# Up projection with tokens on partitions, turned back by block transposes on VectorE

## The chip, the cores and the metric

The kernel runs on one core of one Trainium2 chip. The metric is the device time of one execution in microseconds (us). Before the change, three runs took 2050.69, 2050.99 and 2053.95 us; the median is 2050.99 us. A core has five engines with queues of their own, each working its instructions in order: TensorE (PE, matrix products; its weight loads are shown as PEld), VectorE (DVE), ScalarE (ACT), GpSimd (POOL) and SyncE (SP), which here issues the DMA transfers of the weights. Engines wait for one another by semaphores.

## The reference

One layer of a streaming encoder is computed for 384 tokens: a prompt of 256 frames and 8 streams of 16 new frames. The change lies in the last part, a feed-forward block with a gate and a short convolution over time:

```python
h2 = rmsnorm(x, norm_ffn_g)
up = h2 @ w_up                       # 2048 -> 2 * 5632
g_half = up[..., :D_FF]
u_half = up[..., D_FF:]
ext_f = jnp.concatenate([ffn_buf.astype(g_half.dtype), g_half], axis=1)
gc = causal_dwconv(ext_f, ffn_dw_w, ffn_dw_b)     # 3 taps along time
x = x + (jax.nn.silu(gc) * u_half) @ w_down       # 5632 -> 2048
new_ffn = ext_f[:, -(FFN_CONV_W - 1):]
```

The row factor of `rmsnorm` is one number per token. It commutes with the projection, so the kernel multiplies it in behind the matmuls; the factors of `norm_ffn_g` are in the activations already.

## The kernel before

All matrix products are taken in split precision. A weight tile `raw` (128 partitions × 2 × 512 fp32 numbers, that is two contraction steps of 128 rows and 512 columns) is fetched by SyncE (`fetch`, L117). ScalarE rounds it to `hi` (L124) and VectorE subtracts to get the rest, `lo` (L125). Activations are kept as such a pair too. Each product is three matmuls: hi·hi, hi·lo and lo·hi. `raw` has three buffers, `hi` and `lo` two each. In this document a weight pair is one such tile: two contraction steps.

`gemm` runs jobs. A job makes 512 output columns over `nk` contraction steps, in one of two kinds:

- kind A: the weights are the stationary operand, 128 columns of them at a time, and the 384 tokens stream past. Four PSUM tiles of 128 features × 384 tokens come out: features on partitions. A step takes 4 × 3 = 12 matmuls of 384 columns.
- kind B: the activations are the stationary operand, 128 tokens at a time, and 512 weight columns stream past. Three PSUM tiles of 128 tokens × 512 features come out: tokens on partitions. A step takes 3 × 3 = 9 matmuls of 512 columns.

PSUM has five tiles for this (`acc`). At the job's last step its `evac` functions read the PSUM tiles, and `done` puts further work behind them. The order of TensorE is that of the program; the other engines' orders come from a scheduler that gives the weight splits (`SPLIT_AHEAD`) and the evacuations (`EVAC_AHEAD`) precedence over the rest, so that splits stand between the instructions of an evacuation on VectorE and ScalarE.

The feed-forward part runs 11 groups of 512 features. `up_jobs(g)` gives two jobs of 16 steps (8 weight pairs) each, both kind A: the g job (gate half) and the u job (other half). After some groups come the down jobs (`down_jobs`, kind B) of the groups that are done: `FFN_PLAN` runs five groups up, four down, four up, four down, two up and the last three down.

In the g job's evacuation VectorE multiplies each PSUM tile by the row factors `rs2` (L871), which have been spread over all partitions by matmuls with ones (`over_partitions`, L283), and writes it into `extf`: 24 pieces of 16 tokens, each with two places ahead of it for the two tokens before. GpSimd fills these places, from the neighbouring piece (L873) or from the stored state `sfT` (L874). Then VectorE makes the three taps (L888 for the first, L890 for the other two), ScalarE applies SiLU (L892), GpSimd multiplies by the row factors of the other half (L893) and copies the last tokens for the new state (L894). In the u job VectorE multiplies the PSUM tile by that gate (L910), ScalarE rounds the product to `hi` (L912) and VectorE subtracts to get `lo` (L913): the activations of the down projection.

Of the kernel before, what the change touches and what calls it, by code (L numbers as in the profile page):

```python
# [8 lines left out]
F32 = mybir.dt.float32  # L9
F32R = mybir.dt.float32r  # L10
AF = mybir.ActivationFunctionType
# [4 lines left out]
P = 128  # L16
# [23 lines left out]
def hybrid_step(  # L40
# [33 lines left out]
    def f(ap):  # L74
        return ap.bitcast(F32)
# [34 lines left out]

    # ------------------------------------------------------------------ weight streaming
    def fetch(srcs):
# [51 lines left out]
    def after(units, fn):  # L164
        later.append([units, fn])
# [216 lines left out]

    # ------------------------------------------------------------------ log forget gates
    def tiny(name):
# [61 lines left out]

    # ------------------------------------------------------------------ q, k norms
    def head_rsqrt(a):
# [19 lines left out]

    # ------------------------------------------------------------------ attention
    p_att, close_att = pool("att", side="right")  # L470
# [136 lines left out]

    # ------------------------------------------------------------------ GLU
    ut = gp.tile([P, 8, NT], F32, tag="G4", name="ut")
# [80 lines left out]

    # ------------------------------------------------------------------ gates, conv branch
    p_hl, close_hl = pool("attHL", side="right")
# [20 lines left out]

    # ------------------------------------------------------------------ LayerNorm + swish, att_out
    def layer_norm():
# [60 lines left out]

    # ------------------------------------------------------------------ pointwise, mix
    mix = [gp.tile([P, 2, 4, NT], F32R, tag=f"G{g}", name=f"mix{g}") for g in range(4)]
# [18 lines left out]

    # ------------------------------------------------------------------ w_out, residual, second norm
    p_r, close_r = pool("resid", side="right")
    y = p_r.tile([P, NTT, DM], F32, name="y")  # L800
    xg = [p_r.tile([P, 2, 4, NT], F32R, name=f"xg{g}") for g in range(4)]
    rs2 = p_r.tile([P, NT], F32, name="rs2")
    ss2 = p_r.tile([P, NTT, 4], F32, name="ss2")
# [29 lines left out]
    def second_norm():  # L833
        m2 = p_f.tile([P, NTT], F32, name="m2")
        nc.vector.tensor_reduce(m2[:], ss2[:], axis=mybir.AxisListType.X, op=ALU.add)
        ts(m2[:], m2[:], 1.0 / DM, EPS, op0=ALU.mult, op1=ALU.add)
        r2 = rsqrt(m2[:], [P, NTT], p_f, "r2")
        dg = diagonals(p_f, r2, "r2")
        after(2, lambda: over_partitions(dg, rs2[:]))

    gemm([job("B", 16, grouped(mix), wo_evac(n), done=wo_done(n)) for n in range(4)])

    # ------------------------------------------------------------------ FFN
    sfT = p_f.tile([P, 44, 16], F32, name="sfT")
    sfv = sfT[:].rearrange("p (c i) r -> p c i r", i=11)
    sf_in = state_ffn[0].rearrange("b r (c p) -> (b r c) p", p=P).rearrange("(q i) p -> q i p", i=11)
    for u, i0 in enumerate(range(0, 11, 3)):
# [11 lines left out]
        after(2 + 2 * u, ffn_state)  # L859
    extf = [p_f.tile([P, 24, 18], F32, name=f"extf{m}") for m in range(4)]  # L860
    for m in range(4):
        nc.gpsimd.memset(extf[m][:, 0, 0:2], 0.0)
    xa = grouped(xg)
    acts = {}

    def up_g_evac(g, sg):
        def ev(m, ps):
            c = 4 * g + m
            e = extf[m]
            v = e[:, :, 2:18]  # L870
            tt(v, ps[:, :NT].rearrange("p (a t) -> p a t", t=16), rs2[:].rearrange("p (a t) -> p a t", t=16),  # L871
               op=ALU.mult)
            nc.gpsimd.tensor_copy(e[:, 1:16, 0:2], e[:, 0:15, 16:18])  # L873
            nc.gpsimd.tensor_copy(e[:, 16:24, 0:2], sfT[:, c, :].rearrange("p (b r) -> p b r", r=2))  # L874
        return ev

    def up_g_done(g, sg):
        def done():
            gcs = [p_f.tile([P, NT], F32, tag="gc", bufs=4, name="gc") for _ in range(4)]
            lc = p_f.tile([P, 18, 4], F32, tag="lc", bufs=2, name="lc")  # L880
            for w in range(3):
                for m in range(4):
                    c = 4 * g + m
                    o = gcs[m][:].rearrange("p (a t) -> p a t", t=16)
                    v = extf[m][:, :, w:w + 16]
                    wc = fw[:, w * 44 + c:w * 44 + c + 1]
                    if w == 0:
                        ts(o, v, wc, col[:, R_FDB + c:R_FDB + c + 1], op0=ALU.mult, op1=ALU.add)  # L888
                    else:
                        stt(o, v, wc, o, op0=ALU.mult, op1=ALU.add)  # L890
            for m in range(4):
                nc.scalar.activation(gcs[m][:], gcs[m][:], AF.Silu)  # L892
                nc.gpsimd.tensor_tensor(sg[m][:], gcs[m][:], rs2[:], op=ALU.mult)  # L893
                nc.gpsimd.tensor_copy(lc[:, :, m].rearrange("p (a r) -> p a r", r=2), extf[m][:, 15:24, 16:18])  # L894

            def new_state():
                ps = misc_tile()
                tr(ps[:72, :P], lc[:].rearrange("p a m -> p (a m)"), ident[:])
                nf = p_f.tile([72, P], F32, tag="nf", bufs=2, name="nf")
                nc.scalar.copy(nf[:], ps[:72, :P])  # L900
                cs = slice(512 * g, 512 * (g + 1))
                nc.sync.dma_start(prompt_ffn[0, 0, :, cs].rearrange("r (m p) -> r m p", m=4), nf[0:8, :])
                nc.sync.dma_start(sample_ffn[0, :, :, cs].rearrange("b r (m p) -> (b r) m p", m=4), nf[8:72, :])
            after(10, new_state)
        return done

    def up_u_evac(g, sg):
        def ev(m, ps):
            a = p_f.tile([P, NT], F32, tag="ac", bufs=2, name="ac")
            tt(a[:], ps[:, :NT], sg[m][:], op=ALU.mult)  # L910
            hi, lo = acts[g][:, 0, m, :], acts[g][:, 1, m, :]
            nc.scalar.copy(hi, a[:])  # L912
            tt(lo, a[:], f(hi), op=ALU.subtract)  # L913
        return ev

    def up_jobs(g):
        sg = [p_f.tile([P, NT], F32, tag="sg", bufs=6, name="sg") for _ in range(4)]
        acts[g] = gp.tile([P, 2, 4, NT], F32R, tag=f"G{g % 5}", name=f"act{g}")
        return [job("A", 16, xa, up_g_evac(g, sg), done=up_g_done(g, sg)), job("A", 16, xa, up_u_evac(g, sg))]

# [59 lines left out]
```

## Time and profile before

| what | value |
|---|---|
| median of three runs | 2050.99 us |
| span of the profiled execution, first to last instruction | 2050.9 us |
| TensorE busy | 2035.2 us (99%) |
| VectorE busy | 1046.1 us (51%) |
| ScalarE busy | 723.9 us (35%) |
| GpSimd busy | 225.8 us (11%) |
| moved by DMA | 276.19 MB, mean 135 GB/s |
| matmuls of the up projection, 384 columns | 3 lines (L203 to L205) × 1408 |
| matmuls of the down projection, 512 columns | 3 lines (L208 to L210) × 528 |
| mean clock granted to TensorE | 0.998 of full speed |

The profiled execution's time is its span, 2050.9 us, which stands within 0.1 us of the median: next to nothing lies around it. A row of a group of instructions reads: line, engine, operation, output <- inputs by the program's names, shapes, count | busy us in all, mean ns of one | idle time of the engine just before them, and what ended most of it. A row of a timeline reads: start in us from the span's start, length, engine, line, operation, and in brackets the idle time before it and what ended it. Several like instructions in a row are merged, with their count; the length is then from the first one's start to the last one's end. Instructions of one engine overlap: one can start before the last one's end, and a few records of matmuls can be missing.

### The profile page before, as it was taken

Reading aid. Unit: us, or ns where it says so; the run is one execution under the profiler, and the core shown is the slowest. Engines: PE = TensorE matmul, PEld = TensorE weight load, DVE = VectorE, ACT = ScalarE, POOL = GpSimd, SP = SyncE. Lnnn points to the kernel's source line nnn. Section 1 sums busy time; section 2 is a strip of 40 time slices with the busy share of each in tenths; the row PEclk is TensorE's granted clock in tenths of the full one; section 3 lists DMA queues with packets and bytes.
Section 4 is the critical chain, followed back from the end, with each engine's and each line's share of the span. In section 5 each row is a group of like instructions: output and inputs, shape, how many; then the busy total and the mean of one; then the engine's idle time right before and its main releaser. Section 6 shows DMA issues by size and latency. Waiting matters only on the chain.

```text
span 2050.9 us, 27732 instructions
## 1 busy us (share of the span) xinstructions
PE 2035.2 (99%) x11198; PEld 1909.6 (93%) x11198; DVE 1046.1 (51%) x1413; ACT 723.9 (35%) x1071; POOL 225.8 (11%) x309
## 2 busy tenths in 40 slices
PE   8999999999999999999999999999999999999999
PEld 8988999999999999888999999888999998899987
DVE  4434477778872556344544454433544453335443
ACT  5334455433333433333322332222323332223222
POOL 2000011112120013000221122000220120002100
PEclk9999999999999999999999999999999999999999
DMA  6555465344444344534444444444444444444443
GB/s 179 170 168 159 146 166 162 101 127 119 127 125 125 122 124 125 201 124 121 121 130 124 128 131 124 129 128 133 126 124 130 128 124 133 124 134 124 126 152 124
DMA packets 171214, 276.19 MB, mean 135 GB/s; under 512 B 10841, under 2 KB 58224, under 8 KB 170694
## 3 DMA queue, kind: packets, MB, share of 16 engines
q1 hardware_dynamic: 170542, 273.62, 44.8%
q8 instruction: 87, 1.43, 0.3%
q0 software_dynamic: 512, 0.80, 0.2%
q14 instruction: 41, 0.34, 0.0%
q10 hardware_dynamic: 32, 0.01, 0.0%
HBM read 266.98 MB, written 7.86 MB: 134 GB/s over the span
## 4 chain that ended last, share of the span: by engine, by line
PE 96%; DVE 2%; POOL 1%; DMA 1%; ACT 0%; issue 0%; POOLq 0%; ACTq 0%
PE acc L205 20%; PE acc L203 20%; PE acc L204 20%; PE acc L209 11%; PE acc L210 11%; PE acc L208 11%; DVE ut L663 1%; DVE lo L125 1%; DMA raw<-in_w_in_dram 1%; POOL sgA L710 1%; PE misc L513 0%; PE misc L819 0%; PE misc L579 0%; PE misc L546 0%; POOL sgB L710 0%
## 5 line engine op out<-in xcount | busy, mean ns | idle before, releaser
L125 DVE TENSOR_TENSOR lo<-raw,hi 128x1024 fp32r<-128x1024 f32 (+1 forms) x480 | 588.4, 1226 | 899.3 <-ACT hi L124 894.1
L124 ACT CAST hi<-raw 128x1024 fp32r<-128x1024 f32 (+1 forms) x480 | 497.8, 1037 | 1127.6 <-PE acc L204 665.1
L203 PE MATMUL acc<-xg,hi 128*128 128x384 f32 x1408 | 474.9, 337 | 0.0
L205 PE MATMUL acc<-xg,lo 128*128 128x384 f32 x1408 | 473.1, 336 | 0.0
L204 PE MATMUL acc<-xg,hi 128*128 128x384 f32 x1408 | 473.1, 336 | 0.0
L203 PEld LDWEIGHTS acc<-xg,hi 128*128 128x128 f32 x1408 | 264.7, 188 | 1.4
L204 PEld LDWEIGHTS acc<-xg,hi 128*128 128x128 f32 x1408 | 264.8, 188 | 0.1
L205 PEld LDWEIGHTS acc<-xg,lo 128*128 128x128 f32 x1408 | 264.7, 188 | 0.0
L205 PE MATMUL acc<-hT,lo 128*128 128x384 f32 x768 | 259.8, 338 | 4.8 <-DVE lo L125 4.8
L203 PE MATMUL acc<-hT,hi 128*128 128x384 f32 x768 | 262.5, 342 | 0.0
L204 PE MATMUL acc<-hT,hi 128*128 128x384 f32 x768 | 257.7, 336 | 0.0
L209 PE MATMUL acc<-lo,act 128*128 128x512 f32 x528 | 205.4, 389 | 0.0
L210 PE MATMUL acc<-hi,act 128*128 128x512 f32 x528 | 205.4, 389 | 0.0
L208 PE MATMUL acc<-hi,act 128*128 128x512 f32 x528 | 205.4, 389 | 0.0
L663 DVE SCALAR_TENSOR_TENSOR ut<-ext,cw,ut 128x384 f32<-128x384 f32 x240 | 165.2, 688 | 6.1
L205 PEld LDWEIGHTS acc<-hT,lo 128*128 128x128 f32 x768 | 144.7, 188 | 9.2 <-DVE lo L125 8.5
L203 PEld LDWEIGHTS acc<-hT,hi 128*128 128x128 f32 x768 | 144.7, 188 | 2.2 <-issue 1.4
L204 PEld LDWEIGHTS acc<-hT,hi 128*128 128x128 f32 x768 | 144.9, 189 | 0.0
L208 PE MATMUL acc<-hi,hT 128*128 128x512 f32 (+1 forms) x336 | 123.0, 366 | 2.9 <-ACT hi L124 2.9
L209 PE MATMUL acc<-lo,hT 128*128 128x512 f32 (+1 forms) x336 | 121.4, 361 | 0.7 <-DVE lo L125 0.7
L210 PE MATMUL acc<-hi,hT 128*128 128x512 f32 (+1 forms) x336 | 121.4, 361 | 0.0
L208 PEld LDWEIGHTS acc<-hi,act 128*128 128x128 f32 x528 | 99.1, 188 | 20.7
(290 smaller groups left out, 2119.8 us busy)
## 6 DMA issues: line engine op xcount, KB each, us to landing
raw<-in_w_up_dram SPq DMA_DIRECT2D x176, 512.0 KB
raw<-in_w_in_dram SPq DMA_DIRECT2D x96, 512.0 KB
raw<-in_w_down_dram SPq DMA_DIRECT2D x88, 512.0 KB
raw<-in_w_in_dram SPq DMA_DIRECT2D x64, 256.0 KB
raw<-in_w_out_dram SPq DMA_DIRECT2D x32, 512.0 KB
raw<-in_w_in_dram SPq DMA_DIRECT2D x24, 344.0 KB
raw<-in_w_att_out_dram SPq DMA_DIRECT2D x16, 512.0 KB
raw<-in_conv_pw_out_dram SPq DMA_DIRECT2D x16, 512.0 KB
```

The costliest lines, as they stand in the source:

```text
L124: nc.scalar.copy(hi[:, :, :o], raw[:, :, :o])
L125: tt(lo[:, :, :o], raw[:, :, :o], f(hi[:, :, :o]), op=ALU.subtract)
L203: mm(o, hi[:, kk, s], ah, start=st, stop=False)
L204: mm(o, hi[:, kk, s], al, start=False, stop=False)
L205: mm(o, lo[:, kk, s], ah, start=False, stop=sp)
L208: mm(o, ah[:, s], hi[:, kk, :n], start=st, stop=False)
L209: mm(o, ah[:, s], lo[:, kk, :n], start=False, stop=False)
L210: mm(o, al[:, s], hi[:, kk, :n], start=False, stop=sp)
L663: stt(o, v, wc, o, op0=ALU.mult, op1=ALU.add)
L710: nc.gpsimd.tensor_tensor(d, d, rs1b[:], op=ALU.mult)
```

## The change

Both up jobs become kind B. ScalarE evacuates each PSUM tile (128 tokens × 512 features) into a buffer `tok` in SBUF and multiplies by the row factor on the way, which is now a number per partition; `rs2` shrinks to one column per 128 tokens and isn't spread over partitions any more. Since both halves get their factor there, L893 goes. Then VectorE turns `tok` into features on partitions. Its transpose works on square blocks of 32 × 32: one instruction reads 32 partitions (32 tokens of each of the three token tiles, in 4 × 3 blocks) and writes 32 other partitions; 16 of them, 4 quarters of the features × 4 quarters of the tokens, turn one job's tile. The g half is written into `extf`, the u half into a new buffer `uT`. The work behind stays: carried tokens on GpSimd, taps on VectorE, SiLU, product, split. `extf` is one tile for the four feature blocks in place of four tiles, and `tok` and `uT` have one buffer each.

```diff
@@ second_norm @@
         r2 = rsqrt(m2[:], [P, NTT], p_f, "r2")
-        dg = diagonals(p_f, r2, "r2")
-        after(2, lambda: over_partitions(dg, rs2[:]))
+        nc.vector.tensor_copy(rs2[:], r2[:])
@@ FFN @@
-    extf = [p_f.tile([P, 24, 18], F32, name=f"extf{m}") for m in range(4)]
+    extf = p_f.tile([P, 4, 24, 18], F32, name="extf")
...
-    def up_g_evac(g, sg):
-        def ev(m, ps):
-            c = 4 * g + m
-            e = extf[m]
-            v = e[:, :, 2:18]
-            tt(v, ps[:, :NT].rearrange("p (a t) -> p a t", t=16), rs2[:].rearrange("p (a t) -> p a t", t=16),
-               op=ALU.mult)
-            nc.gpsimd.tensor_copy(e[:, 1:16, 0:2], e[:, 0:15, 16:18])
-            nc.gpsimd.tensor_copy(e[:, 16:24, 0:2], sfT[:, c, :].rearrange("p (b r) -> p b r", r=2))
+    def tok_rows():
+        return p_f.tile([P, NTT, 512], F32, tag="tok", bufs=1, name="tok")
+
+    def up_evac(rows):
+        def ev(t, ps):
+            nc.scalar.activation(rows[:, t, :], ps[:], AF.Identity, scale=rs2[:, t:t + 1])
         return ev
 
-    def up_g_done(g, sg):
+    def blocks(rows, put):
+        src = rows[:].rearrange("p t (m b j) -> p b m t j", m=4, b=4)
+        for b in range(4):
+            for a in range(4):
+                nc.vector.transpose(put(a, slice(32 * b, 32 * b + 32)), src[32 * a:32 * a + 32, b])
+
+    def up_g_done(g, rows, sg):
         def done():
+            def put(a, js):
+                return extf[js].rearrange("p m (t a) c -> p m t a c", t=NTT)[:, :, :, 2 * a:2 * a + 2, 2:18]
+
+            blocks(rows, put)
...
+            for m in range(4):
+                e = extf[:, m]
+                nc.gpsimd.tensor_copy(e[:, 1:16, 0:2], e[:, 0:15, 16:18])
+                nc.gpsimd.tensor_copy(e[:, 16:24, 0:2], sfT[:, 4 * g + m, :].rearrange("p (b r) -> p b r", r=2))
...
             for m in range(4):
-                nc.scalar.activation(gcs[m][:], gcs[m][:], AF.Silu)
-                nc.gpsimd.tensor_tensor(sg[m][:], gcs[m][:], rs2[:], op=ALU.mult)
-                nc.gpsimd.tensor_copy(lc[:, :, m].rearrange("p (a r) -> p a r", r=2), extf[m][:, 15:24, 16:18])
+                nc.scalar.activation(sg[m][:], gcs[m][:], AF.Silu)
+                nc.gpsimd.tensor_copy(lc[:, :, m].rearrange("p (a r) -> p a r", r=2), extf[:, m, 15:24, 16:18])
...
-    def up_u_evac(g, sg):
-        def ev(m, ps):
-            a = p_f.tile([P, NT], F32, tag="ac", bufs=2, name="ac")
-            tt(a[:], ps[:, :NT], sg[m][:], op=ALU.mult)
-            hi, lo = acts[g][:, 0, m, :], acts[g][:, 1, m, :]
-            nc.scalar.copy(hi, a[:])
-            tt(lo, a[:], f(hi), op=ALU.subtract)
-        return ev
+    def up_u_done(g, rows, sg):
+        def done():
+            uT = p_f.tile([P, 4, NT], F32, tag="uT", bufs=1, name="uT")
+            blocks(rows, lambda a, js: uT[js].rearrange("p m (t a i) -> p m t a i", t=NTT, a=4)[:, :, :, a])
+            for m in range(4):
+                tt(uT[:, m], uT[:, m], sg[m][:], op=ALU.mult)
+                hi, lo = acts[g][:, 0, m, :], acts[g][:, 1, m, :]
+                nc.scalar.copy(hi, uT[:, m])
+                tt(lo, uT[:, m], f(hi), op=ALU.subtract)
+        return done
 
     def up_jobs(g):
...
-        return [job("A", 16, xa, up_g_evac(g, sg), done=up_g_done(g, sg)), job("A", 16, xa, up_u_evac(g, sg))]
+        gr, ur = tok_rows(), tok_rows()
+        return [job("B", 16, xa, up_evac(gr), done=up_g_done(g, gr, sg)),
+                job("B", 16, xa, up_evac(ur), done=up_u_done(g, ur, sg))]
```

In the changed file the lines that follow have new numbers: the evacuation is L870, the transposes L877, GpSimd's copies L889 (from the neighbouring piece), L890 (from the stored state) and L903 (for the new state), the taps L898 (first) and L900, SiLU L902, the product L921, its rounding L923 and its rest L924.

More of the change, by code (lines that the diff above doesn't have):

```diff
@@ L801, in hybrid_step @@
     xg = [p_r.tile([P, 2, 4, NT], F32R, name=f"xg{g}") for g in range(4)]
-    rs2 = p_r.tile([P, NT], F32, name="rs2")
+    rs2 = p_r.tile([P, NTT], F32, name="rs2")
     ss2 = p_r.tile([P, NTT, 4], F32, name="ss2")
@@ L859, in hybrid_step @@
         after(2 + 2 * u, ffn_state)
-    extf = [p_f.tile([P, 24, 18], F32, name=f"extf{m}") for m in range(4)]
+    extf = p_f.tile([P, 4, 24, 18], F32, name="extf")
     for m in range(4):
-        nc.gpsimd.memset(extf[m][:, 0, 0:2], 0.0)
+        nc.gpsimd.memset(extf[:, m, 0, 0:2], 0.0)
     xa = grouped(xg)
     acts = {}
-    def up_g_evac(g, sg):
-        def ev(m, ps):
-            c = 4 * g + m
-            e = extf[m]
-            v = e[:, :, 2:18]
-            tt(v, ps[:, :NT].rearrange("p (a t) -> p a t", t=16), rs2[:].rearrange("p (a t) -> p a t", t=16),
-               op=ALU.mult)
-            nc.gpsimd.tensor_copy(e[:, 1:16, 0:2], e[:, 0:15, 16:18])
-            nc.gpsimd.tensor_copy(e[:, 16:24, 0:2], sfT[:, c, :].rearrange("p (b r) -> p b r", r=2))
-        return ev
-    def up_g_done(g, sg):
+    def tok_rows():
[3 more added lines that the diff above has]
+            nc.scalar.activation(rows[:, t, :], ps[:], AF.Identity, scale=rs2[:, t:t + 1])
+        return ev
+    def blocks(rows, put):
[4 more added lines that the diff above has]
+    def up_g_done(g, rows, sg):
         def done():
+            def put(a, js):
+                return extf[js].rearrange("p m (t a) c -> p m t a c", t=NTT)[:, :, :, 2 * a:2 * a + 2, 2:18]
+            blocks(rows, put)
+            lc = p_f.tile([P, 18, 4], F32, tag="lc", bufs=2, name="lc")
             gcs = [p_f.tile([P, NT], F32, tag="gc", bufs=4, name="gc") for _ in range(4)]
-            lc = p_f.tile([P, 18, 4], F32, tag="lc", bufs=2, name="lc")
+            for m in range(4):
+                e = extf[:, m]
+                nc.gpsimd.tensor_copy(e[:, 1:16, 0:2], e[:, 0:15, 16:18])
+                nc.gpsimd.tensor_copy(e[:, 16:24, 0:2], sfT[:, 4 * g + m, :].rearrange("p (b r) -> p b r", r=2))
             for w in range(3):
@@ L884, in done @@
                     o = gcs[m][:].rearrange("p (a t) -> p a t", t=16)
-                    v = extf[m][:, :, w:w + 16]
+                    v = extf[:, m, :, w:w + 16]
                     wc = fw[:, w * 44 + c:w * 44 + c + 1]
```

## The prediction

> **What bounds the kernel now.** I read the page's first table, then the chain of waits, then the timeline of each engine around one group of the up projection, and last the groups of instructions by shape.
>
> ```profile
> PE 2035.2 (99%) x11198; PEld 1909.6 (93%) x11198; DVE 1046.1 (51%) x1413; ACT 723.9 (35%) x1071; POOL 225.8 (11%) x309
> ...
> PE 96%; DVE 2%; POOL 1%; DMA 1%; ACT 0%; issue 0%; POOLq 0%; ACTq 0%
> ...
> SPq L117 <- DVE lo L125: 827.1, 228, 4.6
> ```
>
> TensorE (PE) bounds it: 99% busy, 96% of the chain. In the up stage it never waits, so what counts is how fast matmuls follow one another and whether another engine makes it late. The last row is from the waits of the DMA queue: it waits for VectorE (DVE) to free a weight buffer, so the weights come early and DMA has room.
>
> The timeline of TensorE gives the pace, first in the up projection (384 columns), then in a down projection (512 columns):
>
> ```profile
> 1252.25 0.34 PE L205 MATMUL acc<-xg,lo 128*128 128x384 f32 x1
> 1252.43 0.34 PE L203 MATMUL acc<-xg,hi 128*128 128x384 f32 x1
> 1252.60 0.34 PE L204 MATMUL acc<-xg,hi 128*128 128x384 f32 x1
> ...
> 1323.89 0.39 PE L210 MATMUL acc<-hi,act 128*128 128x512 f32 x1
> 1324.12 0.39 PE L208 MATMUL acc<-hi,act 128*128 128x512 f32 x1
> 1324.35 0.39 PE L209 MATMUL acc<-lo,act 128*128 128x512 f32 x1
> ```
>
> Starts are 0.173 us apart with 384 columns and 0.227 with 512. The durations overlap; only the distance of starts counts. The difference, 0.0533 us for 128 columns, makes 0.160 for 384, so every matmul also carries about 0.013 us that doesn't depend on its width.
>
> The timeline of VectorE (then ScalarE, ACT) shows the clock that each weight pair keeps. One pair is one 512 KB fetch, two contraction steps:
>
> ```profile
> 1184.25 1.23 DVE L125 TENSOR_TENSOR lo<-raw,hi 128x1024 fp32r<-128x1024 f32 x1 [2.94 <-ACT hi L124]
> 1185.94 2.12 DVE L871 TENSOR_TENSOR extf<-acc,rs 128x384 f32<-128x384 f32 x4 [0.46 <-PE acc L205]
> 1187.97 0.47 DVE L888 TENSOR_SCALAR gc<-extf,fw,col 128x384 f32<-128x384 f32 x1
> 1188.41 1.23 DVE L125 TENSOR_TENSOR lo<-raw,hi 128x1024 fp32r<-128x1024 f32 x1
> 1189.56 1.25 DVE L888 TENSOR_SCALAR gc<-extf,fw,col 128x384 f32<-128x384 f32 x3
> 1190.72 2.20 DVE L890 SCALAR_TENSOR_TENSOR gc<-extf,fw,gc 128x384 f32<-128x384 f32 x4
> 1192.84 1.22 DVE L125 TENSOR_TENSOR lo<-raw,hi 128x1024 fp32r<-128x1024 f32 x1
> 1193.98 2.98 DVE L890 SCALAR_TENSOR_TENSOR gc<-extf,fw,gc 128x384 f32<-128x384 f32 x4
> 1197.25 1.67 DVE L125 TENSOR_TENSOR lo<-raw,hi 128x1024 fp32r<-128x1024 f32 x1 [0.29 <-ACT hi L124]
> ...
> 1242.62 1.23 DVE L125 TENSOR_TENSOR lo<-raw,hi 128x1024 fp32r<-128x1024 f32 x1 [2.93 <-ACT hi L124]
> 1246.78 1.23 DVE L125 TENSOR_TENSOR lo<-raw,hi 128x1024 fp32r<-128x1024 f32 x1 [2.94 <-ACT hi L124]
> ...
> 1324.32 1.05 ACT L124 CAST hi<-raw 128x1024 fp32r<-128x1024 f32 x1 [3.02 <-PE acc L210]
> ...
> 1325.40 1.22 DVE L125 TENSOR_TENSOR lo<-raw,hi 128x1024 fp32r<-128x1024 f32 x1 [2.85 <-ACT hi L124]
> 1329.49 1.23 DVE L125 TENSOR_TENSOR lo<-raw,hi 128x1024 fp32r<-128x1024 f32 x1 [2.86 <-ACT hi L124]
> ```
>
> A pair takes 4.16 us in the up projection (24 matmuls of 0.1733) and 4.08 in the down projection (18 of 0.2267). The first nine rows are the burst at a job's end: VectorE works it off between the splits of L125 and no split comes too late. That room is what the change spends. The casts and splits run one pair ahead, since `hi` and `lo` have two buffers: the cast for the next pair starts 0.20 us after this pair's first matmul (1324.32 against 1324.12), its split 1.08 later, and is done 2.51 us after that matmul.
>
> **The change, part by part.** *Matmuls.* All 22 up jobs go from 12 matmuls of 384 columns a step to 9 of 512: the same columns, a quarter fewer matmuls. With 8 pairs a job that is 176 pairs × (4.16 − 4.08) = **−14.1 us**, all on the bounding engine.
>
> *Norm scale.* `over_partitions` goes from the second norm:
>
> ```profile
> 978.09 0.34 PE L205 MATMUL acc<-xg,lo 128*128 128x384 f32 x1
> 978.27 0.83 PE L283 MATMUL misc<-r2d,ones 128*128 128x128 f32 x6
> ...
> 979.12 0.34 PE L204 MATMUL acc<-xg,hi 128*128 128x384 f32 x1
> ```
>
> L204 came 1.03 us after L205 where two steps of 0.173 would do: **−0.7 us**. The small VectorE and ScalarE work beside it was hidden.
>
> *Evacuation.* Six ScalarE activations of 128x512 a group replace L871 and the PSUM read of L910. The groups by shape give all prices:
>
> ```profile
> L871 DVE TENSOR_TENSOR extf<-acc,rs 128x384 f32<-128x384 f32 x44 | 23.3, 558 | 5.1 <-PE acc L205 5.1
> L927 DVE TENSOR_TENSOR y<-acc,y 128x512 f32<-128x512 f32 x36 | 24.6, 692 | 9.0 <-PE acc L210 9.0
> L890 DVE SCALAR_TENSOR_TENSOR gc<-extf,fw,gc 128x384 f32<-128x384 f32 x88 | 56.1, 700 | 0.0
> L893 POOL TENSOR_TENSOR sg<-gc,rs 128x384 f32<-128x384 f32 x44 | 59.9, 1390 | 12.6 <-ACT gc L892 12.6
> L370 ACT ACTIVATE kt<-acc,rs 128x512 f32<-128x512 f32 x4 | 2.7, 680 | 3.3 <-PE acc L210 3.3
> ```
>
> 0.68 us each, the third behind the cast of pair 1, so it ends at 0.23 + 1.05 + 0.68, about 1.9 us after the next job's first matmul. VectorE is then still in the split of pair 1 (until 2.51), which hides it; without that cover the block transposes would start up to 0.6 us earlier, no more. ScalarE idles 3 us a pair (bracket of its row), so its casts stay punctual. The next job has its three PSUM tiles free: five exist, three are used. POOL's L893 goes, off the path.
>
> *The transposes.* This is the cost: 16 of 32 partitions × 384 elements in each job, 352 in all, on VectorE. No row of before shows one. In the changed program VectorE's order after a job is: split 1, 7 transposes, split 2, 6 transposes, split 3, 3 transposes, then in a g job the four L898, split 4, five L900, split 5; in a u job three L921, split 4, three L924, one L921, split 5. What counts is the distance from one transpose to the next.
>
> Bounds from the rows: below, the L888 rows, 0.39 apart (1.25 − 0.47 over 2), or the L871 row, 0.52 apart ((2.12 − 0.56)/3), where an instruction starts before the last has ended; above, the 0.70 of L890 plus a full serial gap. That gap shows where each VectorE instruction needs the one before:
>
> ```profile
> 40.04 0.18 DVE L99 RECIPROCAL r1r<-r1s 128x3 f32<-128x3 f32 x1 [1.15 <-ACT r1s L98]
> 40.25 0.16 DVE L100 TENSOR_TENSOR r1s<-r1r 128x3 f32<-128x3 f32 x1
> ```
>
> 0.03 us from end to start. I take a plain 384-element instruction (0.558, L871) run serially: 0.558 + 0.03 = **0.59 us**. Nearest is the chained row, because every transpose reads another quarter of the partitions than the one before, while all overlapping rows keep to the same 128; and a block must be full before its first output row exists.
>
> The walk, zero at the next job's first matmul. `lo` of pair n is needed by the second matmul of the pair, at 4.08n + 0.23 − 0.03.
> - Split 1 from 1.28; the next instruction enters 1.15 us behind it (1188.41 to 1189.56), at 2.46. Seven transposes end at 6.6.
> - Split 2, 6.6 to 7.82, needed 8.36: in time. Six transposes, 7.86 to 11.4.
> - Split 3, 11.4 to 12.63, needed 12.44: TensorE waits 0.2. Three transposes, to 14.43.
> - In a g job L898 waits for POOL's L889 copy, which waits for the last transpose:
>
> ```profile
> 1186.63 0.21 POOL L873 COPY extf<-extf 128x30 f32<-128x30 f32 x1 [52.55 <-DVE extf L871]
> ```
>
> The first L871 began at 1185.94 and lasted 0.56, so POOL began 0.13 after its end; with 0.21 and 0.03 the L898s start at 14.80, last 4 × 0.39 and split 4 runs 16.36 to 17.58. It was needed at 16.72 (shifted by the 0.2): 0.86 more. **1.06 us a g job.** The L890 copies wait only for the last group's convolution and are long done. Split 5 (20.15 to 21.37, needed 21.66) is in time again.
> - In a u job three L921 at 0.52 put split 4 at 16.0 to 17.22: 0.2 + 0.5 = **0.71 us a u job**; split 5 is in time.
>
> Eleven groups: 11 × 1.77 = **+19.5 us**. A split that is up to 2.4 us later also frees its `raw` buffer later; a fetch is issued three pairs ahead and lands inside that (SP's wait for VectorE, above, is the evidence), so I price it at nothing; the cover gone would be DMA time on TensorE at each job. Last, the final down job reads `act` of group 10 from its ninth step; the late L924 costs about 0.25 once.
>
> Sum against the profiled execution, whose span of 2050.9 is the median of the three runs (2050.99) within 0.1: 2050.9 − 14.1 − 0.7 + 19.5 + 0.25 = **2056 us**. Each 0.01 us in the transpose's distance is 16 × 0.01 a job, 22 jobs: 3.5 us. Below 0.577 us the change wins; below about 0.52 nothing waits.
>
> The Trainium skill, "VectorE: DVE Perf Modes", section "The three transpose paths", gives 311 ns for a 128×128 bf16 block transpose; an estimate from that figure, with 256 more elements at the 1.05 ns each between L871 and L927, is 0.58 us, serially 0.61, and the sum would be 2063. No run here shows it yet.
>
> **Rivals.**
> 1. *Transposes overlap* as L871 does, 0.52 us apart or less (0.54 costs little). For it: every unchained pair of VectorE rows overlaps. Against: the changing partitions. All splits are in time, 2050.9 − 14.8 = **2036 us**; decides below 0.577.
> The Trainium skill, "VectorE: DVE Perf Modes", section "Two Vector instructions with no wait between them", speaks against this rival: an instruction whose first input starts in another quarter of the partitions than the last one's is held until all before it have finished. No row of before shows such a pair.
> 2. *Near the break-even*, 0.565 to 0.589 apart: the two terms cancel, 2047 to 2055.
> 3. *Each block fills, then drains*, with no overlap inside the instruction: 384 elements cost twice 0.40 (1.05 ns each, L871 to L927), 0.96 + 0.03 = 0.99 us. Waits grow by 32 × 0.40 = 12.8 us a group, (1.77 + 12.8) × 11 = 160: **2196 us**. Nothing in the trace speaks for it but that no transpose is in it. The dear end of the rows, 0.73, gives (1.77 + 32 × 0.14) × 11 = 69: 2105.
> 4. *The matmuls gain nothing*, because the activations become the stationary side. The down rows have that form and run at 0.227; I give it no chance of its own.
>
> **How the numbers follow.** A measurement of this kernel can tell a change of about 0.2%, 4.1 us, from none. Overlapping or nearly so, up to 0.565: 0.30, faster. Near the break-even: 0.15, the same (the forecast's own edge reaches into slower at 0.589). Serial, 0.589 to 0.75: 0.40, 2055 to 2110, its likeliest part 2055 to 2070. Above that, towards rival 3: 0.15. The predicted time is that of the serial case by rows, 2056. The range 2036 to 2110 takes in the overlapping case and the dear end of the rows and leaves out 0.15 above and little below.
>
> **What would show it.** Matmuls of xg with 512 columns, 0.227 apart; the transposes at L877 and their distance, 0.59; TensorE waits ended by `lo` L125 in the third and fourth pair of each job, some 20 us in all; group time near 67.0 us (before: 16 × 4.16 = 66.6) where 65.3 would be free of waits; POOL without L893. A distance at or below 0.55 makes the prediction wrong towards 2036; one above 0.75, or splits held up by something else (POOL's copies, late fetches), makes it wrong upwards.

## The result and the profile after

The changed kernel takes 2068.68 us (median of five runs, 2066.53 to 2069.50) where the kernel before takes 2053.95 us beside it (2050.69 to 2054.38). The ratio is 1.0078, with a 95% interval of 1.0066 to 1.0089: slower, by about 16 us. The profiled execution has a span of 2064.8 us, 13.9 more than before's 2050.9.

The changed kernel's page: the busy line of each engine, the chain of waits, and the groups of the `lo` matmul in the up and in the down projection.

```profile
PE 2044.5 (99%) x10136; PEld 1767.5 (86%) x10136; DVE 1205.1 (58%) x1719; ACT 767.7 (37%) x1136; POOL 161.7 (8%) x265
...
PE 85%; DVE 10%; issue 2%; ACT 1%; POOL 1%; DMA 1%; POOLq 0%; ACTq 0%
...
L209 PE MATMUL acc<-lo,xg 128*128 128x512 f32 x1056 | 419.3, 397 | 3.8 <-DVE lo L125 3.8
...
L209 PE MATMUL acc<-lo,act 128*128 128x512 f32 x528 | 206.1, 390 | 0.2
```

TensorE has 1062 instructions fewer (10136 for 11198), and the span is longer. The chain goes through VectorE for 10% of the span (2% before): nearly all of that is the burst of transposes and what stands in line with it. And the same matmul, 512 columns of `lo` weights, lasts 397 ns with `xg` as the stationary operand and 390 with `act`. The timeline of TensorE, first in the up projection, then in a down projection, shows what that does to the distance of starts:

```profile
1182.77 0.40 PE L208 MATMUL acc<-hi,xg 128*128 128x512 f32 x1
1183.00 0.40 PE L209 MATMUL acc<-lo,xg 128*128 128x512 f32 x1
...
1184.87 0.40 PE L208 MATMUL acc<-hi,xg 128*128 128x512 f32 x1
...
1323.73 0.39 PE L210 MATMUL acc<-hi,act 128*128 128x512 f32 x1
1323.96 0.39 PE L208 MATMUL acc<-hi,act 128*128 128x512 f32 x1
...
1325.09 0.39 PE L210 MATMUL acc<-hi,act 128*128 128x512 f32 x1
```

In the up projection nine distances make 2.10 us, 0.2333 each; in the down projection six make 1.36, 0.2267. A weight pair, 18 matmuls, takes 4.20 us in the up projection and not 4.08. Before it took 4.16. So the fewer matmuls cost 176 × (4.20 − 4.16) = 7.0 us more.

VectorE's timeline in the changed kernel, the burst behind a u job's matmuls and the end of the one behind the next g job's:

```profile
1156.67 1.23 DVE L125 TENSOR_TENSOR lo<-raw,hi 128x1024 fp32r<-128x1024 f32 x1 [2.98 <-ACT hi L124]
1157.82 4.04 DVE L877 STREAM_TRANSPOSE uT<-tok 32x384 f32<-32x384 f32 x7
1161.89 1.23 DVE L125 TENSOR_TENSOR lo<-raw,hi 128x1024 fp32r<-128x1024 f32 x1
1163.15 3.49 DVE L877 STREAM_TRANSPOSE uT<-tok 32x384 f32<-32x384 f32 x6
1166.67 1.22 DVE L125 TENSOR_TENSOR lo<-raw,hi 128x1024 fp32r<-128x1024 f32 x1
...
1186.15 1.23 DVE L125 TENSOR_TENSOR lo<-raw,hi 128x1024 fp32r<-128x1024 f32 x1 [2.97 <-ACT hi L124]
1190.35 1.23 DVE L125 TENSOR_TENSOR lo<-raw,hi 128x1024 fp32r<-128x1024 f32 x1 [2.97 <-ACT hi L124]
...
1201.61 1.74 DVE L877 STREAM_TRANSPOSE extf<-tok 32x384 f32<-32x384 f32 x3
1203.73 1.72 DVE L898 TENSOR_SCALAR gc<-extf,fw,col 128x384 f32<-128x384 f32 x4 [0.38 <-POOL extf L889]
1205.37 1.21 DVE L125 TENSOR_TENSOR lo<-raw,hi 128x1024 fp32r<-128x1024 f32 x1
```

Seven transposes in 4.04 us, the next instruction right behind: they stand 0.58 apart, one after the other. Two splits 4.20 apart, 1186.15 and 1190.35, show the pair's length where nothing is late. TensorE's timeline where it waits for the last of these splits:

```profile
1205.87 0.40 PE L208 MATMUL acc<-hi,xg 128*128 128x512 f32 x1
1206.64 0.50 PE L209 MATMUL acc<-lo,xg 128*128 128x512 f32 x1 [0.38 <-DVE lo L125]
```

That is a late split: 0.77 from start to start where 0.233 would do, 0.54 lost. (The bracket counts only from the modelled end of the last matmul, so it shows less than is lost.) To add up such losses, every distance between successive up-projection matmuls that exceeds the usual one by over 0.03 us is taken, and its excess summed. In the following this sum is called the late time. It is 9.0 us in the changed kernel (49 distances) and 1.8 before (20), where no split of this stage's groups is late: 0.8 lies in the first 25 us of the stage, and one distance a group is some 0.09 too long in every kernel here. The down projection, counted in the same way, loses 1.8 us in the changed kernel (13 distances) and nothing before: the bursts of the three u jobs that a down projection follows end there.

By these rows the change costs +7.0 us by the pace of the matmuls, +7.2 and +1.8 by late operands in the up and the down projection, and −0.7 by the norm's matmuls: +15.3. From the start of the first up matmul to that of the last down matmul the traces have 1096.4 us before (949.9 to 2046.3) and 1111.9 after (948.2 to 2060.1), 15.5 more. That the span grew by only 13.9 is since the stages ahead, which are the same, took 1.7 us less in this execution; in the other runs here the first up matmul starts between 947.6 and 951.4. What was open: why a matmul of the same shape is slower with `xg`, and whether the late splits come from the transposes alone.

### The profile page after: what moved, and what is told of

Same layout as the page of the kernel before. It is cut to its first block, busy times and chain, and to the rows that moved or that the text cites. A ratio compares the mean times of both kernels' runs of the same rounds, so it can differ in the third digit from the quotient of the medians.

```text
span 2064.8 us, 25830 instructions
## 1 busy us (share of the span) xinstructions
PE 2044.5 (99%) x10136; PEld 1767.5 (86%) x10136; DVE 1205.1 (58%) x1719; ACT 767.7 (37%) x1136; POOL 161.7 (8%) x265
## 4 chain that ended last, share of the span: by engine, by line
PE 85%; DVE 10%; issue 2%; ACT 1%; POOL 1%; DMA 1%; POOLq 0%; ACTq 0%
PE acc L209 20%; PE acc L210 19%; PE acc L208 19%; PE acc L205 8%; PE acc L203 8%; PE acc L204 8%; DVE extf L877 4%; DVE lo L125 3%; DVE gc L898 1%; ACT hi L124 1%; DVE uT L877 1%; DVE ut L663 1%; DMA raw<-in_w_in_dram 1%; POOL sgA L710 1%; PE misc L513 0%
## 5 line engine op out<-in xcount | busy, mean ns | idle before, releaser
L209 PE MATMUL acc<-lo,xg 128*128 128x512 f32 x1056 | 419.3, 397 | 3.8 <-DVE lo L125 3.8
L208 PE MATMUL acc<-hi,xg 128*128 128x512 f32 x1056 | 419.3, 397 | 0.0
L210 PE MATMUL acc<-hi,xg 128*128 128x512 f32 x1056 | 417.6, 395 | 0.0
L209 PEld LDWEIGHTS acc<-lo,xg 128*128 128x128 f32 x1056 | 198.4, 188 | 56.8 <-DVE lo L125 10.6
L208 PEld LDWEIGHTS acc<-hi,xg 128*128 128x128 f32 x1056 | 198.4, 188 | 48.6
L210 PEld LDWEIGHTS acc<-hi,xg 128*128 128x128 f32 x1056 | 198.4, 188 | 47.1
L209 PEld LDWEIGHTS acc<-lo,act 128*128 128x128 f32 x528 | 99.1, 188 | 22.9 <-DVE lo L125 2.4
```

The lines of the kernel that those rows point to most:

```text
L208: mm(o, ah[:, s], hi[:, kk, :n], start=st, stop=False)
L209: mm(o, ah[:, s], lo[:, kk, :n], start=False, stop=False)
L210: mm(o, al[:, s], hi[:, kk, :n], start=False, stop=sp)
```

## Experiments

### Why the matmuls with xg are slow: its place in SBUF

In the changed kernel the program places `hi`, `lo` and `act` 96 bytes past a multiple of 128 in each partition, and `xg` at a multiple of 128. The change itself moved `xg`: `rs2`, which stands in the same pool at the far end of SBUF, shrank from 1536 bytes a partition to 12, padded to 32, and the tiles of that pool moved by the difference, 1504 bytes. The theory: the pace depends on where the two operands of a matmul lie relative to each other. The rival: on where `xg` lies by itself, or on something else in the up stage (the transposes beside it). Widening `rs2` by 8 columns moves `xg` and the other tiles at that end, the buffers of the transposes among them, by 32 bytes, and leaves the weights; widening `rs1`, which lies ahead of the weight buffers, moves these and leaves `xg` and the buffers of the transposes.

e1, `xg` moved to the weights' place:

```diff
-    rs2 = p_r.tile([P, NTT], F32, name="rs2")
+    rs2 = p_r.tile([P, NTT + 8], F32, name="rs2")
...
-        nc.vector.tensor_copy(rs2[:], r2[:])
+        nc.vector.tensor_copy(rs2[:, :NTT], r2[:])
```

> The changed kernel with rs2 eight columns wider, which moves xg (and the tiles under it) by 32 bytes in SBUF and nothing else: xg then lies at 32 bytes modulo 64, as hi, lo, mix and act do, where it lay at 0. Address theory (matmuls of xg are slow, 0.233 us apart in place of 0.227, for where xg lies): the matmuls of xg come to 0.227 apart, a weight pair to 4.08 us, 3168 x 0.0067 = 21 us less; the waits for late splits rise, because the splits are needed earlier, from about 10 to about 17 us; 2065 - 21 + 7 = 2051 in the profile. Rival, the pace belongs to the stage (its neighbours on other engines, its transfers) or to the far end of SBUF: 0.233 and 2065 as before.

e2, the weights (and `act`) moved to `xg`'s place, and e3, both moved, so that they differ again:

```diff
-    rs1 = cp.tile([P, NTT], F32, name="rs1")
+    rs1 = cp.tile([P, NTT + 8], F32, name="rs1")
...
-        nc.vector.tensor_copy(rs1[:], r[:])
+        nc.vector.tensor_copy(rs1[:, :NTT], r[:])
```

> The changed kernel with rs1 eight columns wider, which moves hi, lo, raw, mix, act and hT by 32 bytes, to 0 modulo 64; xg stays at 0. If it is the difference between the two operands' places that counts: 0.227 in the up, the down and the w_out matmuls. If a stationary operand at 0 is slow by itself: 0.233 in all of them, the down projection too. If it is neither: up 0.233, down 0.227.

> Both shifts: hi, lo, mix, act and hT at 0 modulo 64, xg at 32. Difference counts: up 0.233, down 0.227. A stationary operand at 0 is slow: up 0.227, down 0.233. Neither: up 0.233, down 0.227 as in the changed kernel, which the run before then tells from the first.

e8 and e10 are e1 with `NTT + 24` and `NTT + 16`, to see how the distance counts beyond 32 bytes:

> The changed kernel with rs2 24 columns wider, so that xg begins 64 bytes off the weights' place modulo 128 bytes and at it modulo 64. Theory of a period of 64 bytes: the up stage's matmuls are 0.227 us apart as in e1 and the time is about 2058. Rival, a period of 128 bytes (only equal places are quick): 0.233 and about 2068.

> The changed kernel with rs2 16 columns wider: xg begins 32 bytes past the weights' place modulo 128, where the changed kernel has it 32 bytes short of it (96 past). With 0.227 at distance 0 (e1), 0.229 at 64 (e8) and 0.234 at 96. Theory that the distance counts modulo 128 and is worst when odd in steps of 32: about 0.234 and 2069. Rival (it grows with the distance 0, 32, 64, 96): 0.228 and about 2061.

e9 puts the kernel before into the same difference of places, with `rs2` 8 columns wider (its uses take the first `NT` columns):

```diff
-    rs2 = p_r.tile([P, NT], F32, name="rs2")
+    rs2 = p_r.tile([P, NT + 8], F32, name="rs2")
```

> The kernel before, with rs2 8 columns wider, so that its xg begins 32 bytes off the weights' place modulo 64 bytes; there xg is the 384-column operand and the weights are loaded as 128 columns. Theory that any difference of places between the two operands slows a matmul: by 2 to 3% of the up stage's 4224 matmuls of 0.173 us, 15 to 22 us, so 2066 to 2073 us. Rival (only where the 512-column operand is the weights): 0.173 us apart as before and 2051 us.

What was measured. The place is that of `xg` less that of the weights, modulo 128 bytes; the pace is the mean distance of successive up matmuls, without those that count as late.

| kernel | columns streamed | place | pace, us | late time, us | time, us |
|---|---|---|---|---|---|
| changed | 512 | 32 | 0.2333 | 9.0 | 2068.68 |
| e1 | 512 | 0 | 0.2273 | 18.1 | 2058.49 (2055.16 to 2060.26, 8 runs) |
| e2 | 512 | 0 | 0.2272 | 18.1 | 2058.22 (one run) |
| e3 | 512 | 96 | 0.2333 | 9.0 | 2069.75 (one run) |
| e8 | 512 | 64 | 0.2291 | 15.3 | 2062.70 (one run) |
| e10 | 512 | 96 | 0.2333 | 9.2 | 2069.19 (one run) |
| before | 384 | 64 | 0.1733 | 1.8 | 2051.46 (beside e1) |
| e9 | 384 | 32 | 0.1745 | 1.8 | 2055.21 (one run; before beside it 2051.67) |

The `lo` matmul's group in e1, e8 and e10, by the pages of these kernels:

```profile
L209 PE MATMUL acc<-lo,xg 128*128 128x512 f32 x1056 | 415.6, 394 | 7.2 <-DVE lo L125 6.8
```

```profile
L209 PE MATMUL acc<-lo,xg 128*128 128x512 f32 x1056 | 417.4, 395 | 6.7 <-DVE lo L125 6.4
```

```profile
L209 PE MATMUL acc<-lo,xg 128*128 128x512 f32 x1056 | 418.9, 397 | 4.0 <-DVE lo L125 4.0
```

What follows. Moving either operand so that the places agree gives 0.227, moving both leaves 0.233: it is the difference that counts, not where `xg` lies, and e2 has the buffers of the transposes where the changed kernel has them. Equal is quick, 64 off costs about a third as much as 32 or 96 off, so the period isn't 64. That it is 128 is not shown: no kernel here has the operands an odd multiple of 128 bytes apart. (The expectation of e10 has the two sides swapped: the changed kernel is 32 past, e10 is 96 past. Both sides are equally slow.) The pace of e1 and e2 still has some of the burst in it: in e4 and e6 below, where `xg` lies as in e1 and no split of the stage's groups is late, it is 0.2268, that of the down projection. The kernel before had a difference too, 64; e9, which makes it 32, moves its pace by 0.0011, which is 4.8 us in 4224 matmuls, and its time by 3.5 us in one run, where 15 to 22 was expected of the first theory and none of the rival: neither held. So with 384 columns and the weights as the stationary operand the effect is there but small: the same step, from 64 to 32, makes 0.0042 with 512 columns and 0.0011 here. What inside the chip makes it is not settled here: no view shows the reads of the two operands.

The ratio of e1 to the kernel before is 1.0028 (1.0018 to 1.0039). Its profiled span is 2054.8 us, where 2051 was expected: the pace gained 19 us and not 21, and the late time rose by 9.1 and not 7. The direction of both is what the theory said: the pair became 0.11 us shorter, so every split's deadline moved up, and the late time went from 9.0 to 18.1. The slow matmuls had been hiding half of the burst. VectorE's timeline of e1 in the u job seen above:

```profile
1154.16 1.22 DVE L125 TENSOR_TENSOR lo<-raw,hi 128x1024 fp32r<-128x1024 f32 x1 [2.85 <-ACT hi L124]
1155.30 4.04 DVE L877 STREAM_TRANSPOSE uT<-tok 32x384 f32<-32x384 f32 x7
1159.38 1.23 DVE L125 TENSOR_TENSOR lo<-raw,hi 128x1024 fp32r<-128x1024 f32 x1
1160.63 3.49 DVE L877 STREAM_TRANSPOSE uT<-tok 32x384 f32<-32x384 f32 x6
1164.16 1.22 DVE L125 TENSOR_TENSOR lo<-raw,hi 128x1024 fp32r<-128x1024 f32 x1
```

The burst is as long as in the changed kernel (4.04 and 3.49 again). Only TensorE is quicker beside it, eight distances in 1.82 us, by its timeline:

```profile
1182.74 0.39 PE L208 MATMUL acc<-hi,xg 128*128 128x512 f32 x1
...
1184.56 0.39 PE L210 MATMUL acc<-hi,xg 128*128 128x512 f32 x1
```

### Are the late splits the transposes' doing?

e4 is e1 with the 16 transposes of a job made 4 of 128 partitions. It leaves out the exchange between quarters of the partitions (each block is turned within its own quarter); every other instruction stays.

```diff
         for b in range(4):
-            for a in range(4):
-                nc.vector.transpose(put(a, slice(32 * b, 32 * b + 32)), src[32 * a:32 * a + 32, b])
+            nc.vector.transpose(put(b, slice(0, P)), src[:, b])
```

> As e1, with 4 transposes of 128 partitions a job in place of 16 of 32: each turns its blocks within their quarter of the partitions and none goes to another quarter, so the exchange between quarters is left out and the output is not the reference's. VectorE then has 4 x 0.57 us of transposes a job in place of 16. Theory (the loss beside the matmul pace is late splits behind serial transposes): no TensorE wait in the up stage is ended by a split, and the time is 2051 - 14.1 - 0.7 = 2036. Rival (the waits come from the longer way over ScalarE, GpSimd or from the fetches): waits of some 10 us stay, 2046.

It takes 2038.13 us (2036.74 to 2039.53, four runs), ratio 0.9929 (0.9913 to 0.9946); the late time is 1.8 us, as before. Its chain of waits, by its page:

```profile
PE 96%; DVE 2%; POOL 1%; DMA 1%; ACT 0%; issue 0%; POOLq 0%; ACTq 0%
```

VectorE's share is back at before's 2%. And its groups by shape, from 1000 us on:

```profile
L876 DVE STREAM_TRANSPOSE uT<-tok 128x384 f32<-128x384 f32 x44 | 21.4, 545 | 0.0
```

A transpose of four times the elements lasts 545 ns, less than the narrow one's 569 (below): with 384 columns, 32 partitions cost no less than 128. The burst costs 2058.49 − 2038.13 = 20.4 us at the quick pace.

### Why they are serial

e5 is e1 with each transpose cut in two halves of 192 columns, which read and write the same quarters. e11 is e1 with the two loops swapped, so that four transposes in a row read the same quarter and write different ones.

```diff
-                nc.vector.transpose(put(a, slice(32 * b, 32 * b + 32)), src[32 * a:32 * a + 32, b])
+                for h in (slice(0, 2), slice(2, 4)):
+                    nc.vector.transpose(put(a, slice(32 * b, 32 * b + 32))[:, h], src[32 * a:32 * a + 32, b, h])
```

> e1 with each transpose of 32x384 cut in two of 32x192 (m = 0, 1 and m = 2, 3), 32 a job in the place of 16. Theory of the prediction (serial, each a fixed part of about 0.19 us and the rest by columns): a half takes about 0.38 us and they stand 0.39 us apart whether the next one reads the same quarter or another, 32 x 0.39 = 12.5 us a job in the place of 9.3; the splits are then later by some 20 to 50 us in all, so 2080 to 2110 us. Rival (a transpose that reads other partitions than the one before it is held, and one that reads the same ones is not): first to second half of a quarter about 0.33 us apart, across quarters 0.39.

```diff
-        for b in range(4):
-            for a in range(4):
+        for a in range(4):
+            for b in range(4):
```

> e1 with the two loops over quarters swapped: four transposes in a row read the same quarter of the partitions and write to the four others in turn. In e5 the second half of a transpose, which reads and writes the same quarters as the first, began 0.302 us after it, 0.067 before its end, and the next quarter's 0.340 us after, 0.013 past its end. Theory A (what holds a transpose is that its input starts in another quarter): twelve of fifteen stand about 0.51 us apart in the place of 0.582, the late splits fall by 0.07 x 6 each where 6 stand between two splits, about 18 to 11 us in all, and the time to about 2051. Theory B (the output's quarter holds it as well): 0.582 all through and 2058.

One of VectorE's groups by shape in e5:

```profile
L878 DVE STREAM_TRANSPOSE uT<-tok 32x192 f32<-32x192 f32 x352 | 112.0, 350 | 2.8
```

VectorE's timeline in e5, the first twelve halves behind a u job's matmuls:

```profile
1155.92 3.83 DVE L878 STREAM_TRANSPOSE uT<-tok 32x192 f32<-32x192 f32 x12
```

And the group of whole transposes in e11:

```profile
L877 DVE STREAM_TRANSPOSE uT<-tok 32x384 f32<-32x384 f32 x176 | 100.2, 569 | 2.6
```

In e5 the second half starts 0.302 us after the first (median of 330 such distances), 0.067 before its end; the next quarter's first half 0.340 after (308 distances), 0.014 past the end. The row agrees: 6 × 0.302 + 5 × 0.340 + the last's 0.32 = 3.83. So a transpose overlaps the one before if both keep to the same quarters, and is held if not. e4 agrees for whole ones: its four start at the same quarter and stand 0.46 to 0.50 us apart, less than their 0.545. In e11 the distance is 0.582 where only the output's quarter changes (median of 220) and 0.585 where both change (66), and the late time stays at 17.9 (time 2056.52 in one run): keeping the input's quarter isn't enough, a change of the output's holds it too, theory B. Each of a job's 16 transposes has a pair of quarters of its own, so every order of them is serial. For that overlap, e5's 32 instructions take 3.83 + 3.59 + 2.96 = 10.4 us a job in three stretches, where 12.5 was expected, and its time, 2059.65 us in one run (late time 20.0), is about 1 us above e1's.

### Spreading the burst

e6 is e1 with the same 16 transposes, but queued four behind each of four splits. `split` keeps its last `lo` instruction in `last_lo`; conv, gate and product come behind the fourth group, and the new state's output is moved along. Group 10's u job is left as it was.

```diff
+        def behind_split(b):
+            with tc.issue_after(last_lo[0].ins):
+                quarter(b)
+
         for b in range(4):
-            for a in range(4):
-                nc.vector.transpose(put(a, slice(32 * b, 32 * b + 32)), src[32 * a:32 * a + 32, b])
+            if spread:
+                after(2 * b + 2, lambda b=b: behind_split(b))
+            else:
+                quarter(b)
+        if spread:
+            after(9, then)
+        else:
+            then()
```

> The kernel with xg at the weights' place modulo 64 bytes (e1: matmuls 0.227 us apart, late splits 18.1 us, 2058.49 us), and each job's sixteen transposes recorded four at a time, each four queued behind the lo of one weight pair; conv, gate and product follow after the fourth group. Theory (the splits are late because 6 or 7 transposes of 0.58 us stand between two of them): four of them and a split take 4 x 0.58 + 1.22 = 3.54 us, less than a pair's 4.08, so the late time falls from 18.1 us to about 2 and the time to 2058.5 - 16 = 2042 us, up to about 4 us lower by the step that e4 measured (2038). Rival (the splits are late for another reason, the evacuation of the job on ScalarE ahead of hi, or VectorE's total work of conv and product): the late time stays near 18 us and the time near 2058.

e7 is e6 with `rs2` as the changed kernel has it, so with `xg` 32 bytes off:

> e6 with rs2 as the changed kernel has it, so that xg is again 32 bytes off the weights' place: the transposes are spread, the matmuls are not mended. Theory (two separate causes that add up): late splits about 2 us as in e6 and matmuls 0.234 us apart as in the changed kernel, 2038.7 + 3168 x 0.0067 = 2060 us, which is the changed kernel less its 9.0 us of late splits (2068.7 - 9.0 = 2059.7) and then some 2 us. Rival (the slow matmuls come from the transposes that run beside them, or from the buffers that these keep, and not from the place of xg): 0.227 and 2039.

e6 takes 2038.66 us (2037.87 to 2040.67, five runs); its ratio to the kernel before is 0.9933 (0.9919 to 0.9946). Its chain of waits, by its page:

```profile
PE 95%; DVE 2%; POOL 1%; DMA 1%; ACT 0%; issue 0%; POOLq 0%; ACTq 0%
```

And VectorE's timeline in e6 behind a u job's matmuls:

```profile
1156.62 1.23 DVE L125 TENSOR_TENSOR lo<-raw,hi 128x1024 fp32r<-128x1024 f32 x1 [0.64 <-ACT hi L124]
1157.88 2.32 DVE L879 STREAM_TRANSPOSE uT<-tok 32x384 f32<-32x384 f32 x4
1160.70 1.22 DVE L125 TENSOR_TENSOR lo<-raw,hi 128x1024 fp32r<-128x1024 f32 x1 [0.51 <-ACT hi L124]
1161.96 2.32 DVE L879 STREAM_TRANSPOSE uT<-tok 32x384 f32<-32x384 f32 x4
1164.78 1.22 DVE L125 TENSOR_TENSOR lo<-raw,hi 128x1024 fp32r<-128x1024 f32 x1 [0.50 <-ACT hi L124]
```

VectorE now waits for `hi` ahead of each split, by 0.50 us or more: room instead of lateness. The late time is 1.8 us. The same transposes at the same 0.58 cost nothing in the up projection where they are four to a pair; group 10's u job, which wasn't spread, loses 0.8 us in the down projection. That it is the transposes and not the later place of conv and product is shown together with e4, which leaves those in place and takes as little.

e7 takes 2059.78 us (2057.65 to 2061.73, six runs), ratio 1.0035 (1.0022 to 1.0047), with a pace of 0.2333 and 1.7 us late. The first matmul line of the up projection in e6 and in e7:

```profile
L209 PE MATMUL acc<-hi,xg 128*128 128x512 f32 x1056 | 412.6, 391 | 0.0
```

```profile
L209 PE MATMUL acc<-hi,xg 128*128 128x512 f32 x1056 | 419.3, 397 | 0.0
```

The slow matmuls aren't caused by how the transposes lie beside them, and the two causes are now priced one by one. The place alone: e7 − e6, 21.1 us. The burst alone: e1 − e6, 19.8 us. Both together: changed − e6, 30.0 us and not 40.9, because the slower pace gives the splits more time; behind the slow pace the burst costs 2068.68 − 2059.78 = 8.9 us. With neither, in e6, the change gains 13.0 us on the kernel before (2051.67 beside it). So the change's result, +17 us by that median, is a gain of 13.0 and a loss of 30.0. (The medians of the kernel before lay between 2051.46 and 2053.95 beside the different kernels, and the result by them between +14.7 and +17.2; sums across runs are good to such 2 us.)

## Why the prediction was right and wrong

The direction and the range were right: 2068.68 us lies in 2036 to 2110, in the likeliest part of the serial case, 2055 to 2070. The forecast of 2056 is 12.7 us too low: 3.9 of it is that the median stands above the profiled span of 2064.8, the other 8.8 are in the terms. Of the 3.9, 1.7 lies around the span of an execution (this one took 2066.53, the least of the five) and 2.2 between executions. So the time isn't the span: in a run of the kernel before it is 1.9 more (2052.56 for a span of 2050.7, beside e1), and that its profiled span met its median within 0.1 was chance. Of the two large terms one failed, and the other was, for that reason, not what was measured. That the sum still came as near as it did is in part luck: the two errors have opposite signs.

*Matmuls, −14.1 us: failed.* The step took the pace of the down rows, 0.227, for the up projection, as 176 × (4.16 − 4.08). It was +7.0: 0.2333 apart, 4.20 a pair. Rival 4, "the matmuls gain nothing", came true, though not for the cause that it named (activations as the stationary side), and it had been given no chance of its own. The down rows had the same form and the same shapes, but their operands lie at equal places and those of `xg` don't. The diff shows the cause: `rs2` shrinks, and the tiles of its pool move. Where the places agree, the term is right: from the first up matmul to the last it takes from 951.3 to 1935.5 us in e6 and from 949.9 to 1948.5 before, 14.4 us less, of which 0.7 is the norm's and 13.7 the matmuls'.

*Norm scale, −0.7 us*: right in kind, too small to be tested.

*Evacuation, hidden: right.* In e6, where it runs as in the changed kernel, nothing of it is late. POOL's L893 is gone and wasn't missed.

*Transposes, 0.59 us apart and serial: right.* 0.569 long, 0.58 apart. The choice among far bounds, that the changing quarters make them serial, was the right reading, and e5 and e11 show the reason itself. The Trainium skill, "VectorE: DVE Perf Modes", section "Two Vector instructions with no wait between them", states it for the output's quarter as well as for the first input's; the prediction weighed only the input. e11 agrees with the page: 0.58 us with the input's quarter kept. The estimate that the prediction worked out from the Trainium skill, "VectorE: DVE Perf Modes", section "The three transpose paths", 0.61 apart, was a little high.

*Late splits, +19.5 us: the working right, the sum not.* e1 has nearly the pace that the walk assumed. Of its late time of 18.1 us 16.3 are late splits, and the three u jobs that a down projection follows lose 1.6 there: 17.9, where 19.5 was forecast. By time the burst costs 19.8. The walk's parts show in e1 too: 0.2 us at split 3, 0.89 at split 4 of a g job (0.86 forecast), 0.32 of a u job (0.5 forecast). POOL's copy held L898 by 0.38, as worked out (0.37). But in the changed kernel each pair is 0.12 longer, which by the fourth split gives 0.48 more room: a g job loses 0.62 there and at the matmul behind it, a u job 0.08. Only the three u jobs with a down projection behind them, whose pair is 4.08, lose 0.5 each. The prediction had named what would show this, "group time near 67.0 us": it is 68.0 in the changed kernel (late matmuls at 1138.6 and 1206.6) and 67.3 in e1 (1136.46 and 1203.72).

*Fetches, nothing: right.* DMA has 1% of the chain, as before. (By the walk's own figures split 4 of a g job ends 2.8 us later than it would without the burst, and not 2.4; nothing hung on it.)

*Wait for act of group 10, +0.25: right.* It stands among the weight loads, where `act` is the stationary operand. In the changed kernel's timeline of these (PEld):

```profile
1978.57 0.19 PEld L209 LDWEIGHTS acc<-lo,act 128*128 128x128 f32 x1 [0.49 <-DVE lo L125]
1979.04 0.19 PEld L210 LDWEIGHTS acc<-hi,act 128*128 128x128 f32 x1 [0.28 <-DVE act L924]
```

The two matmuls stand 0.47 apart there, 0.24 more than the usual 0.227.

So there are two errors of opposite sign: 7.0 + 14.1 = 21.1 us too little for the matmuls, 19.5 − 7.2 − 1.6 = 10.7 too much for the late splits. They leave 10.4, and with the 1.7 us that the stages ahead took less, 8.7 of the 8.8. They aren't independent: the slow pace made the one and took away from the other.

## What to carry to other kernels

A pace read from another stage holds for the same shapes at the same places: when a change resizes a buffer, list where the operands behind it go, and look for another distance of starts in the first timeline after it. A burst on an engine that only prepares is priced by what stands between two deadlines, not by its sum; 16 transposes a job that cost 20 us in all as 7, 6 and 3 cost next to nothing as 4, 4, 4 and 4. Two such causes needn't add up, since one that slows the bounding engine gives the other more room; so undo each with the other undone as well.

## What the runs showed of the hardware that was not expected

The distance of matmuls of 512 columns depends on where the stationary and the streamed operand lie in SBUF relative to each other: by the difference modulo 128 bytes, 0.2272 us at 0, 0.2291 at 64, 0.2333 at 32 and 96, whichever of the two is moved, with the granted clock between 0.997 and 0.999 in all of these profiles. That is 2.7% of the distance. With 384 columns, weights stationary, a place of 32 takes 0.1745 where 64 takes 0.1733. What makes it, and whether the period is 128 bytes or more, stays open. The Trainium skill, "SBUF — State Buffer", section "Who interferes with whom", gives TensorE two independent read ports, one for the moving operand and one for the weight load; from that alone one would not expect the pace to depend on both places; here it does, and the measurement decides. A block transpose on VectorE lasts 0.569 us for 32 × 384 fp32 elements, 0.350 for 32 × 192 and 0.545 for 128 × 384.
